# High halves of two weight blocks ahead of their low halves, and a later place for the output function, in the paired products of a streaming-encoder block

## The chip, the cores and the metric

The kernel runs on one core of one Trainium2 chip. The metric is the device time of one execution in microseconds. Three runs of the kernel before took 1686.04, 1686.25 and 1686.39 us; the median is 1686.25. One more execution was recorded by the hardware profiler; all rows below come from it.

The engines are named as in the profile: PE is TensorE's matmul, PEld its weight load, DVE is VectorE, ACT is ScalarE, POOL is GpSimd, SP is SyncE. PEq, SPq, ACTq and POOLq are the sequencers and DMA queues of these engines. L259 is line 259 of the kernel before.

## The reference

One layer of a block on 512 tokens with 2048 channels, all in float32:

```python
h = rmsnorm(x, norm_gain)
proj = h @ w_in
(aq, ak, av, az, iq, ik, iw, rq, rk, rv, rz, ga, gb) = jnp.split(proj, SPLIT_POINTS, axis=-1)
...
a_out = dsa_mixer(aq, ak, av, iq, ik, iw, positions, rel_bias) * jax.nn.silu(az)
...
b_out = retention_mixer(rq, rk, rv, ret_gn_gain) * jax.nn.silu(rz)
merged = jax.nn.sigmoid(ga) * (a_out @ w_a_out) + jax.nn.sigmoid(gb) * (b_out @ w_b_out)
r = x + merged @ w_o
return r + (p_i @ w_ple) * jax.nn.sigmoid(r @ w_ple_gate)
```

`dsa_mixer` is an attention over the top 128 keys of an index score, with a relative bias; `retention_mixer` is a chunkwise retention with rotary queries and keys. A last rmsnorm follows. What matters here is that most of the time goes into plain products of a 2048-wide activation with weight matrices: `w_in` in many column blocks, then `w_a_out`, `w_b_out`, `w_o` and `w_ple_gate`.

## The kernel before, in words

Activations lie with channels on the 128 partitions and the 512 tokens along the free axis. A float32 product is made from rounded parts: a value v is split into a high part (a copy to a rounded type, on ScalarE) and a low part (v minus the high part, on VectorE). `split_to` (L122) does this for weights: ScalarE writes `wh` (L137), and a function `rest` writes `wl` on VectorE (L142). `rest` may also change the raw weights for a later use: it adds another raw block (L144, VectorE) or starts an accumulating load from memory (L105, issued by POOL). `wh` and `wl` have three buffers each, the raw weights seven.

Column blocks are computed two at a time by `gemm_pair` (L214), by a scheme of seven products in place of eight (a Strassen form): the inner dimension has two halves, the two column blocks are the two column halves, and the tokens are the two row halves. The seven weight combinations are units 0 to 6 of the pair, made from four raw blocks in place: `t` is used for units 0, 4 and 5 with sums in between, `w11` for 1 and 6, `w21` for 2, `w22` for 3. The activation side (`X`) has been made before. Each product has eight k steps. A step has one matmul with the high weights over 512 columns (256 of the activation's high part and 256 of its low part) and one with the low weights over 256 columns. Products 0 to 6 accumulate in the banks v, p, q, r, p, v, p of the accumulator memory, where 4, 5 and 6 add to what is there already.

The order of TensorE's work is written out by hand: for each product in turn the eight high matmuls, then the eight low ones; in products 4 and 6 the low ones come first. After a product, its bank is copied by ScalarE (`pv`, `e1`, `e2`, `e3`, L225) or combined with such a copy by VectorE (`out`, L229), and `done` adds the 256-column pieces into the output tiles (L887). There are 40 pairs with `gate_pair` (24 for retention's queries and keys and the merge gates, four for the retention gate, eight for attention's queries and keys, four for its gate) and eight with `w_o`; the first of the eight (`late`) takes the last k step of products 0 and 1 after the others, since its operand is made last.

Every two matmuls `step` (L161) counts a tick. Work that other engines are to do is put into the program at a tick: `later(n, f)` runs `f` n ticks on, `todo` gives one piece a tick, and `bg` one piece every so many ticks (top-k rounds, masks of the bias). A product has eight ticks, a pair 56. Ticks only fix the order in each engine's queue: each engine works through its queue in order and waits where an operand or a buffer is not there yet.

At the start of product n, `split_to` puts the split of the weights two products ahead into the queues, and `load_to` issues raw loads (SyncE, L116) up to seven units ahead. `rest` follows one tick later. When both pieces of an output tile are there, `gate_pair` puts `finish` into the queue one tick later. `finish` is an activation function on ScalarE with a store on ScalarE's own DMA queue (L896, L923), for the retention gate a product and a store on POOL (L910 to L912), and in the pairs of retention's queries and keys a rotation (`rotate`): two copies on ScalarE (L757, L758) and, three, five and seven ticks later, three operations on VectorE (L759 to L761). From the second rotation on retention's own small matmuls are counted (at 24, 39, 51 and 90 ticks after it).

Of the kernel before, what the change touches and what calls it, by code (L numbers as in the profile page):

```python
# [35 lines left out]
def block_kernel(tc, xT, pT, posb, posq, w_in, w_v, w_ik, w_a, w_b, w_o, w_ple, w_gate,  # L36
                 w_gt, w_pt, fgb, tab, gains, cst, dec, out, out_a, out_b):
    nc = tc.nc
    pe, dve, act, pool, sp = nc.tensor, nc.vector, nc.scalar, nc.gpsimd, nc.sync

    with contextlib.ExitStack() as ctx:
# [10 lines left out]
        def U(name, dt=F32):  # L52
            return up.tile([128, L], dt, name=name, tag="u")

        def B(name, dt=F32):
            return bp.tile([128, 1280], dt, name=name, tag="b")

        def P(name):
            return pp.tile([128, L], F32, name=name, tag="p")
# [10 lines left out]
        loaded = {}  # L70
# [29 lines left out]
        def view(t, nk, cols):  # L100
            return t.rearrange("p a c -> p (a c)")[:, 0:nk * cols].rearrange("p (a c) -> p a c", c=cols)

        def add_block(r, b):
            src, k0 = b
            pool.dma_start(out=raw_tiles[r], in_=src[:, k0:k0 + 8, :], accum_op=OP.add)  # L105

        def load_to(n):
            need = max((u[0] for u in units[:n]), default=-1) + 1
            while state["raw"] < need:
                i = state["raw"]  # L110
                src, k0, nk, cols, plus = raws[i]
                if nk * cols <= L and i < 4:
                    t = U("wraw4").rearrange("p (a c) -> p a c", c=128)
                else:
                    t = wp.tile([128, 8, 128], F32, name="wraw", tag="wraw", bufs=RAW_BUFS)
                sp.dma_start(view(t, nk, cols), src[:, k0:k0 + nk, :])  # L116
                raw_tiles[i] = t
                if plus is not None:
                    add_block(i, plus)
                state["raw"] += 1  # L120

        def split_to(n):  # L122
            while state["split"] < min(n, len(units)):
                i = state["split"]
                load_to(i + 1)
                r, plus, nk, cols = units[i]
                if r in unfinished:
                    unfinished[r]()
                raw = view(raw_tiles[r], nk, cols)
                if i in in_raws:  # L130
                    t = wp.tile([128, 2, 512], F32R, name="whl", tag="wraw", bufs=RAW_BUFS)
                    h, l = t[:, 0:1], t[:, 1:2]
                elif nk * cols == L:
                    h, l = (U(n, F32R).rearrange("p (a c) -> p a c", c=cols) for n in ("wh4", "wl4"))
                else:
                    h, l = (view(wp.tile([128, 8, 128], F32R, name=n, tag=n), nk, cols) for n in ("wh", "wl"))
                act.activation(h, raw, AF.Copy)  # L137

                def rest(r=r, plus=plus, l=l, raw=raw, h=h):
                    if unfinished.pop(r, None) is None:  # L140
                        return
                    dve.tensor_sub(l, raw, h.bitcast(F32))  # L142
                    if isinstance(plus, int):
                        dve.tensor_add(raw, raw, view(raw_tiles[plus], nk, cols))  # L144
                    elif plus is not None:
                        add_block(r, plus)

                unfinished[r] = rest
                later(1, rest)
                loaded[i] = (h, l)  # L150
                state["split"] += 1

# [6 lines left out]
        def later(n, f):  # L159
            if n <= 0:  # L160
                return f()  # L161
            tick[1] += 1
            heapq.heappush(soon, (tick[0] + n, tick[1], f))

        def step():
            tick[0] += 1
            while soon and soon[0][0] <= tick[0]:
                heapq.heappop(soon)[2]()
            f = todo.popleft() if todo else None
            if f is not None:  # L170
                f()
            elif bg and tick[0] % state["rate"] == 0:
                bg.popleft()()
# [31 lines left out]
        ALL = slice(0, L)  # L205
# [4 lines left out]

        LO, HI = slice(0, 256), slice(256, 512)
        PRODUCTS = ("s3", "a11", "a12", "s4", "s2", "a22", "s1")

        def gemm_pair(ids, X, done, late=False):  # L214

            p, v, q, r = (P("ps_" + n) for n in ("p", "v", "q", "r"))  # L220
            E = {}

            def copy(n, src):
                E[n] = U(n)
                act.activation(E[n], src, AF.Copy)  # L225

            def out(f, x, y, i, c):
                t = U("e_t")
                f(t, x, y)  # L229
                done(t[:, LO], t[:, HI], i, c)  # L230

            def last():
                copy("e3", p)
                out(dve.tensor_sub, p, E["pv"], 1, HI)
                out(dve.tensor_add, r, E["e3"], 1, LO)

            after = {
                0: lambda: copy("pv", v),
                1: lambda: copy("e1", p),
                2: lambda: out(dve.tensor_sub, q, E["e1"], 0, LO),  # L240
                4: lambda: copy("e2", p),
                5: lambda: out(dve.tensor_sub, v, E["e2"], 0, HI),
                6: last,
            }
            banks = (v, p, q, r, p, v, p)
            runs = [(n, range(8), True) for n in range(7)]
            if late:
                runs[0:2] = [(n, range(7), False) for n in (0, 1)] + [(n, (7,), True) for n in (0, 1)]
            count = 0
            for n, ks, end in runs:  # L250
                i, o = ids[n], banks[n]
                if ks[0] == 0:
                    split_to(i + AHEAD - (late and n == 1))
                    load_to(i + AHEAD + LOADS)
                parts = (1, 0) if n in (4, 6) else (0, 1)
                for part in parts:
                    w, c = loaded[i][part], (ALL, LO)[part]
                    for k in ks:
                        pe.matmul(o[:, c], w[:, k], X[PRODUCTS[n]][k][:, c], start=(n < 4 and part == 0 and k == 0),  # L259
                                  stop=(part == parts[1] and k == 7), skip_group_check=True)  # L260
                        count += 1
                        if count % 2 == 0:
                            step()
                if end and n in after:
                    after[n]()

        def combos(lo, hi, name, keep=None):


            X = {n: [None] * 8 for n in PRODUCTS}  # L270
            T = {}
# [138 lines left out]

        x_split(0)
        split_to(1)
        step()
        x_split(1)
# [254 lines left out]
        hd = dp.tile([56, 128, L], F32, name="hd")  # L669
        x_at = {(n, k): hd[8 * i + k] for i, n in enumerate(PRODUCTS) for k in range(8)}  # L670
        xn = {}
# [10 lines left out]
        _, h_step = combos(lambda k: xn[k], lambda k: xn[k + 8], "h", lambda n, k: x_at[n, k])  # L682
# [168 lines left out]

        Xh = {n: [None] * 8 for n in PRODUCTS}
        x_wanted = collections.deque((n, k) for n in PRODUCTS for k in range(8))

# [25 lines left out]
        def gate_pair(ids, finish):  # L880
            t = B("go")
            outs = [t[:, 0:512], t[:, 512:1024]]
            have = [0, 0]

            def done(c0, c1, i, q):
                o = outs[i]
                dve.tensor_add(o[:, q], c0, c1)  # L887
                have[i] += 1
                if have[i] == 2:
                    later(1, lambda: finish(i, o))  # L890

            gemm_pair(ids, Xh, done)

# [195 lines left out]
        for m in PAIRED:  # L1089
            t = B("sm")  # L1090
            s, o = t[:, 0:512], t[:, 512:1024]
# [17 lines left out]
        for m in range(8):  # L1109
# [9 lines left out]
            def done(c0, c1, i, q, xc=xc):  # L1119
                dve.tensor_add(xc[i][:, q], xc[i][:, q], c0)  # L1120
                dve.tensor_add(xc[i][:, q], xc[i][:, q], c1)
# [14 lines left out]
        for m in range(MF):  # L1136
            i = u_p[m // 4][0]
# [5 lines left out]
            for k in range(2):  # L1143
                a, b = pparts[k]
                w = 2 * (m % 4) + k
# [129 lines left out]
        for i in range(2):  # L1275
            c = (slice(0, 384), slice(384, 512))[i]
# [16 lines left out]
        for q in range(MF // 4):  # L1293
            o = U("yo")
# [6 lines left out]
            o = o.rearrange("p (a c) -> p a c", a=4)  # L1301
# [9 lines left out]
AHEAD = 3  # L1311
LOADS = 5
# [101 lines left out]
```

## Time and profile before

| What | Value |
|---|---|
| median of three runs | 1686.25 us |
| lowest and highest run | 1686.04 and 1686.39 us |
| the profiled execution | 1686.46 us |
| span of the profiled execution, first to last instruction | 1684.7 us |
| mean granted TensorE clock | 0.998 |
| instructions | 24747 |
| stage of the 40 gate pairs | from about 279 us to about 1110 us |
| stage of the eight `w_o` pairs | from about 1318 us to about 1477 us |

How to read the rows. The page gives each engine's busy time with its share of the span, and the chain of work that ended last, followed back from the last instruction, as shares. A row of a group has line, engine, operation, output<-inputs, shapes and count; behind the first bar the busy time in us and the mean of one in ns; behind the second the engine's idle time just before these instructions and what ended it. A row of the timeline has start, length, engine, line, operation, tiles and count of like instructions in a row; a bracket tells of idle time before it and what ended it. Matmuls are pipelined, so the length of a row reaches into the next one, and the pace is read from start to start. A row of the chain has start, length and what, a product's high and low matmuls together (x16); its starts lie a little later than those of the timeline.

### The profile page before, as it was taken

The numbers are of one execution on the slowest core, as the hardware profiler recorded it, in microseconds if no ns is written. First come the engines' busy times: TensorE is split into PE (matmuls) and PEld (weight loads), VectorE is DVE, ScalarE is ACT, GpSimd is POOL, SyncE is SP. The second block draws the span as 40 slices with busy tenths as digits, with TensorE's granted clock in tenths as the row PEclk, the third lists the DMA queues.
The fourth block names the chain that finished last, engine by engine and source line by source line (L and its number), as shares of the span: only waits on it lengthen the run. The fifth ranks groups of instructions, "written<-read, shape, count | busy, mean of one in ns | idle before, by whom it ended". The sixth has DMA issues, their size and how long they took to land.

```text
span 1684.7 us, 24747 instructions
## 1 busy us (share of the span) xinstructions
PE 1672.4 (99%) x9208; PEld 1451.1 (86%) x9208; DVE 1275.3 (76%) x2020; ACT 863.0 (51%) x1278; POOL 214.8 (13%) x216
## 2 busy tenths in 40 slices
PE   9999999999999999999999999999999999999997
PEld 7988888888888888888888888888888888888897
DVE  7797888987878878877876876787768877864453
ACT  7465423555555555555554555566644444463342
POOL 2100000111111111111331111100000111112222
PEclk9999999999999999999999999999999999999999
DMA  7438989788788788788988889898566788733222
GB/s 288 126 107 310 374 298 327 182 229 220 183 219 213 200 215 212 198 213 215 250 237 214 217 206 233 246 368 278 177 200 189 193 229 214 204 116 100 88 63 100
DMA packets 135369, 355.85 MB, mean 211 GB/s; under 512 B 14801, under 2 KB 26961, under 8 KB 135249
## 3 DMA queue, kind: packets, MB, share of 16 engines
q1 hardware_dynamic: 102496, 256.20, 44.3%
q0 software_dynamic: 21376, 77.60, 25.5%
q10 hardware_dynamic: 11376, 20.47, 3.3%
q8 instruction: 72, 1.18, 0.3%
q14 instruction: 49, 0.39, 0.1%
HBM read 301.26 MB, written 52.95 MB: 210 GB/s over the span
## 4 chain that ended last, share of the span: by engine, by line
PE 94%; DVE 2%; ACT 1%; DMA 1%; issue 1%; POOL 0%; SPq 0%; POOLq 0%; ACTq 0%; DVEq 0%
PE ps_p L259 23%; PE ps_v L259 16%; PE ps_r L259 8%; PE ps_q L259 8%; PE ps_vn L726 3%; PE ps_vn L727 3%; PE ps_vn L728 3%; PE ps_w L198 3%; PE ps_w L197 3%; PE ps_w L199 3%; PE ps_pg L199 3%; PE ps_pg L197 3%; PE ps_pg L198 3%; PE ps_iq L197 1%; PE ps_iq L199 1%; PE ps_iq L198 1%
## 5 line engine op out<-in xcount | busy, mean ns | idle before, releaser
L142 DVE TENSOR_TENSOR wl<-wraw,wh 128x1024 fp32r<-128x1024 f32 (+2 forms) x459 | 562.1, 1232 | 201.7 <-ACT wh L137 198.4
L137 ACT ACTIVATE wh<-wraw 128x1024 fp32r<-128x1024 f32 (+2 forms) x459 | 474.1, 1042 | 283.5 <-DVE wraw L144 129.3
L105 POOL DMA_DIRECT2D wraw<-w_in x120 | 106.3, 960 | 837.6 <-DVE wl L142 264.3
L225 ACT ACTIVATE e<-ps_p 128x512 f32<-128x512 f32 x144 | 86.1, 598 | 158.6 <-PE ps_p L259 151.5
L259 PE MATMUL ps_p<-hs,wh 128*128 128x512 f32 x640 | 161.3, 394 | 0.0
L259 PEld LDWEIGHTS ps_p<-hs,wh 128*128 128x128 f32 x640 | 114.9, 189 | 21.2 <-issue 0.7
L726 PE MATMUL ps_vn<-wh,hh 128*128 128x512 f32 x256 | 99.8, 390 | 0.0
L727 PE MATMUL ps_vn<-wl,hh 128*128 128x512 f32 x256 | 99.7, 390 | 0.0
L728 PE MATMUL ps_vn<-wh,hl 128*128 128x512 f32 x256 | 99.7, 389 | 0.0
L259 PE MATMUL ps_p<-hs,wl 128*128 128x256 f32 x640 | 92.0, 284 | 0.7 <-DVE wl L142 0.7
L259 PEld LDWEIGHTS ps_p<-hs,wl 128*128 128x128 f32 x640 | 83.0, 192 | 1.4 <-DVE wl L142 0.9
L259 PE MATMUL ps_r<-hs,wh 128*128 128x512 f32 x320 | 82.2, 395 | 0.0
L259 PE MATMUL ps_v<-ha,wh 128*128 128x512 f32 x320 | 80.6, 393 | 0.0
L259 PE MATMUL ps_p<-ha,wh 128*128 128x512 f32 x320 | 80.4, 393 | 0.0
L259 PE MATMUL ps_q<-ha,wh 128*128 128x512 f32 x320 | 80.1, 392 | 0.0
L259 PE MATMUL ps_v<-hs,wh 128*128 128x512 f32 x320 | 79.6, 390 | 0.1
L199 PE MATMUL ps_pg<-rh,wl 128*128 128x512 f32 x192 | 74.8, 390 | 0.0
L197 PE MATMUL ps_pg<-rh,wh 128*128 128x512 f32 x192 | 74.7, 389 | 0.0
L198 PE MATMUL ps_pg<-rl,wh 128*128 128x512 f32 x192 | 74.7, 389 | 0.0
L887 DVE TENSOR_TENSOR go<-e_t 128x256 f32<-128x256 f32 x160 | 68.1, 425 | 5.6
L259 PEld LDWEIGHTS ps_v<-hs,wh 128*128 128x128 f32 x320 | 59.8, 188 | 13.2 <-ACT wh L137 0.5
L259 PEld LDWEIGHTS ps_v<-ha,wh 128*128 128x128 f32 x320 | 59.3, 188 | 12.5 <-issue 0.5
(361 smaller groups left out, 3499.4 us busy)
## 6 DMA issues: line engine op xcount, KB each, us to landing
wraw<-w_in SPq DMA_DIRECT2D x172, 512.0 KB, 5.5
wraw<-w_in POOLq DMA_DIRECT2D x120, 512.0 KB, 8.4
wraw<-w_v SPq DMA_DIRECT2D x32, 512.0 KB, 5.0
wraw<-w_o SPq DMA_DIRECT2D x32, 512.0 KB, 5.1
wraw<-w_o POOLq DMA_DIRECT2D x24, 512.0 KB, 6.7
wraw<-w_gate SPq DMA_DIRECT2D x24, 512.0 KB, 4.1
hd<-hs SPq DMA_DIRECT2D x32, 256.0 KB, 5.2
hs<-hd SPq DMA_DIRECT2D x32, 256.0 KB, 5.4
```

What stands on the lines that cost most here:

```text
L105: pool.dma_start(out=raw_tiles[r], in_=src[:, k0:k0 + 8, :], accum_op=OP.add)
L137: act.activation(h, raw, AF.Copy)
L142: dve.tensor_sub(l, raw, h.bitcast(F32))
L197: pe.matmul(o, h[:, k, w], a, start=(s == order[0]), stop=False)
L198: pe.matmul(o, h[:, k, w], b, start=False, stop=False)
L199: pe.matmul(o, l[:, k, w], a, start=False, stop=(s == order[-1]))
L225: act.activation(E[n], src, AF.Copy)
L259: pe.matmul(o[:, c], w[:, k], X[PRODUCTS[n]][k][:, c], start=(n < 4 and part == 0 and k == 0), stop=(part == parts[1] and k == 7), skip_gr ...
L726: pe.matmul(pss[t], a[:, tok(t)], h[:, k], start=(s == 0), stop=False)
L727: pe.matmul(pss[t], a[:, tok(t)], l[:, k], start=False, stop=False)
L728: pe.matmul(pss[t], b[:, tok(t)], h[:, k], start=False, stop=(s == KT - 1))
L887: dve.tensor_add(o[:, q], c0, c1)
```

## The change

In `gemm_pair` the high matmuls of products 0 and 1 come first, then their low ones; the same for products 2 and 3. Products 4, 5 and 6 keep their order. The places at which splits are put into the queues are a table (`SPLIT_AT`, by number of the run of eight matmuls), and so are those of the loads. The split for product 3 stands ahead of the low matmuls of product 0, with its low half five ticks behind instead of one. The split for product 5 stands ahead of the low matmuls of product 3, where it stood ahead of the high ones. In the pair marked `late` the last k step of products 0 and 1 follows the same order. In `gate_pair` the function on a finished tile comes five ticks behind the last sum instead of one.

```diff
-        def split_to(n):
+        def split_to(n, lag=1):
...
-                later(1, rest)
+                later(lag, rest)
...
+        RUNS = [(n, part) for part, ns in enumerate(((0, 1), (0, 1), (2, 3), (2, 3, 4), (4, 5), (5, 6), (6,)))
+                for n in ns]
+        RUNS = [(n, part % 2) for n, part in RUNS]
+
+        SPLIT_AT = {0: 3, 2: 4, 3: 4, 4: 5, 7: 6, 8: 7, 10: 8, 12: 9}
+        LOAD_AT = (0, 2, 4, 6, 8, 10, 12)
...
-            runs = [(n, range(8), True) for n in range(7)]
+            runs = [(n, part, range(8)) for n, part in RUNS]
             if late:
-                runs[0:2] = [(n, range(7), False) for n in (0, 1)] + [(n, (7,), True) for n in (0, 1)]
+                runs[0:4] = [(n, part, ks) for ks in (range(7), (7,)) for n, part, _ in runs[0:4]]
+            ended = [0] * 7
             count = 0
-            for n, ks, end in runs:
+            for at, (n, part, ks) in enumerate(runs):
+                at = max(at - 4, 0) if late else at
                 i, o = ids[n], banks[n]
-                if ks[0] == 0:
-                    split_to(i + AHEAD - (late and n == 1))
-                    load_to(i + AHEAD + LOADS)
-                parts = (1, 0) if n in (4, 6) else (0, 1)
-                for part in parts:
-                    w, c = loaded[i][part], (ALL, LO)[part]
-                    for k in ks:
-                        pe.matmul(o[:, c], w[:, k], X[PRODUCTS[n]][k][:, c], start=(n < 4 and part == 0 and k == 0),
-                                  stop=(part == parts[1] and k == 7), skip_group_check=True)
-                        count += 1
-                        if count % 2 == 0:
-                            step()
-                if end and n in after:
+                if at in SPLIT_AT and not (late and at == 2):
+                    split_to(ids[0] + SPLIT_AT[at], 5 if at == 2 else 1)
+                if at in LOAD_AT:
+                    load_to(ids[LOAD_AT.index(at)] + AHEAD + LOADS)
+                w, c = loaded[i][part], (ALL, LO)[part]
+                first = ended[n] == 0
+                for k in ks:
+                    ended[n] += 1
+                    pe.matmul(o[:, c], w[:, k], X[PRODUCTS[n]][k][:, c], start=(n < 4 and first and k == 0),
+                              stop=(ended[n] == 16), skip_group_check=True)
+                    count += 1
+                    if count % 2 == 0:
+                        step()
+                if ended[n] == 16 and n in after:
                     after[n]()
...
                 if have[i] == 2:
-                    later(1, lambda: finish(i, o))
+                    later(5, lambda: finish(i, o))
```

## The prediction

> **What bounds the kernel now.** I read the busy shares on the page first, then the chain of work that ended last, then the groups of instructions.
>
> ```profile
> PE 1672.4 (99%) x9208; PEld 1451.1 (86%) x9208; DVE 1275.3 (76%) x2020; ACT 863.0 (51%) x1278; POOL 214.8 (13%) x216
> ...
> PE 94%; DVE 2%; ACT 1%; DMA 1%; issue 1%; POOL 0%; SPq 0%; POOLq 0%; ACTq 0%; DVEq 0%
> ...
> L142 DVE TENSOR_TENSOR wl<-wraw,wh 128x1024 fp32r<-128x1024 f32 (+2 forms) x459 | 562.1, 1232 | 201.7 <-ACT wh L137 198.4
> ```
>
> TensorE is busy 99% of the span and carries 94% of the chain. VectorE comes next, at 76%, and its largest work is the low halves of weights (L142). The reader is to see that only two things can move the time: TensorE's own pace, and a new wait of TensorE for a weight half. The view of line 259, the products of a pair, tells how much waiting there is to remove:
>
> ```profile
>   issue: 3.0, 9
>   DVE wl L142: 1.9, 3
>   ACT wh L137: 0.5, 1
>   DVE e_t L229: 0.4, 1
> ```
>
> That is under 6 us over 48 pairs, weight loads counted beside the matmuls. So the first part of the change has to be judged by the pace of matmuls that never wait. The timeline of TensorE over one pair with no other matmuls in it:
>
> ```profile
> 868.17 1.98 PE L259 MATMUL ps_v<-hs,wh 128*128 128x512 f32 x8
> 869.98 1.11 PE L259 MATMUL ps_v<-hs,wl 128*128 128x256 f32 x8
> 870.93 2.00 PE L259 MATMUL ps_p<-ha,wh 128*128 128x512 f32 x8
> 872.78 1.11 PE L259 MATMUL ps_p<-ha,wl 128*128 128x256 f32 x8
> 873.73 2.00 PE L259 MATMUL ps_q<-ha,wh 128*128 128x512 f32 x8
> ...
> 879.32 1.12 PE L259 MATMUL ps_p<-hs,wl 128*128 128x256 f32 x8
> 880.27 2.00 PE L259 MATMUL ps_p<-hs,wh 128*128 128x512 f32 x8
> 882.12 1.98 PE L259 MATMUL ps_v<-ha,wh 128*128 128x512 f32 x8
> 883.93 1.12 PE L259 MATMUL ps_v<-ha,wl 128*128 128x256 f32 x8
> ```
>
> Matmuls overlap, so a run of eight is measured from its start to the start of the next. A high run behind a high run (868.17, and 882.12) takes 1.81 us. A high run behind a low run (870.93) takes 1.85 and (880.27) 1.85. Low runs take 0.95 us behind a high run (869.98, 872.78) and as much behind a low one (879.32). So what a run costs depends a little on its neighbour. These differences are near the last digit of the view; the chain over the same pair adds a high and a low run in each row and serves as a second reading:
>
> ```profile
> 865.53 2.80 PE ps_p L259 x16
> 868.33 2.77 PE ps_v L259 x16
> 871.10 2.79 PE ps_p L259 x16
> 873.89 2.79 PE ps_q L259 x16
> 876.68 2.79 PE ps_r L259 x16
> 879.48 2.80 PE ps_p L259 x16
> 882.28 2.77 PE ps_v L259 x16
> 885.04 2.80 PE ps_p L259 x16
> ```
>
> From 871.10 to 879.48 three products, each a high run behind a low one and a low run behind a high one, take 8.38 us, 2.793 each. The products at 868.33 and 882.28 (high behind high, low behind high) take 2.77 and 2.76, mean 2.765. Those at 865.53 and 879.48 (low behind low, then high behind low) take 2.80 each.
>
> **The order of the runs.** Name a run by product and half: 0h is the high run of product 0. Before: 0h 0l 1h 1l 2h 2l 3h 3l 4l 4h 5h 5l 6l 6h. After: 0h 1h 0l 1l 2h 3h 2l 3l and then the same six. No matmul is added or taken away. Runs 1h and 3h come to stand behind a high run instead of a low one: by the chain each gains 2.793 - 2.765 = 0.028 us. Runs 1l and 3l come to stand behind a low run instead of a high one: each loses 2.80 - 2.793 = 0.007. Net 0.02 us for each of two places in 48 pairs: 2 x 48 x 0.02 = **1.9 us** off the path. The bounds are those of the readings: by single chain rows, 0.02 - 0.01 gives 0.01 a place and 1.0 us in all; by the timeline, 0.03 to 0.04 less nothing gives up to 3.8 us. I take 0.02, from the longest stretch.
>
> The Trainium skill, "TensorE: Matmul & The Clock Gate", Part 2, Step-by-step (① LDWEIGHTS), speaks against this part: the next weights load while this matmul runs, over a read port of their own, so a matmul's neighbours would not matter and the order would be worth nothing. The 1.81 beside 1.85 us above speaks against the rule at this fine a scale.
>
> **The splits that move.** With the 1.81, 1.85 and 0.95 us above, 3h starts 7.4 us after its pair's start instead of 8.4 and 1h 1.8 instead of 2.8: their high halves must be there 1 us earlier. Low run 2l starts 9.2 us in instead of 7.4, so that low half has more time, and 4l to 6h keep theirs. What the halves have to spare, from ScalarE's timeline of the same pair and VectorE's:
>
> ```profile
> 868.86 1.05 ACT L137 ACTIVATE wh<-wraw 128x1024 fp32r<-128x1024 f32 x1
> 871.25 0.63 ACT L910 ACTIVATE go<-go 128x512 f32<-128x512 f32 x1 [1.33 <-DVE go L887]
> 871.78 0.58 ACT L225 ACTIVATE pv<-ps_v 128x512 f32<-128x512 f32 x1
> 872.26 1.05 ACT L137 ACTIVATE wh<-wraw 128x1024 fp32r<-128x1024 f32 x1
> ...
> 884.13 1.06 ACT L137 ACTIVATE wh<-wraw 128x1024 fp32r<-128x1024 f32 x1 [0.27 <-PE ps_v L259]
> ```
>
> ```profile
> 873.58 1.21 DVE L142 TENSOR_TENSOR wl<-wraw,wh 128x1024 fp32r<-128x1024 f32 x1
> ```
>
> The high half for 3h (872.26) is done at 873.31, 5.1 us into the pair. After the change it even stands ahead of the copy `pv` (0.58 us) in ScalarE's queue. Spare: at least 7.4 - 5.1 = 2.3 us. That for the next pair's 1h (884.13) is done at 885.19 and wanted at 868.17 + 19.5 (the seven rows of the chain from 868.33 on) + 1.81 = 889.5, 4.3 us later. The low half for 3l is moved five steps back. In its buffer lies the low half of product 0, which TensorE now reads until about 4.6 us into the pair (1.81 + 1.81 + 0.95) instead of 2.8. VectorE gets to it at 873.58, 5.4 us in, so that the new wait has passed; behind it stand the low half for 4l and the sum `t += w21`, for which the split for 5h waits. Cost in such pairs: nothing; were VectorE to come 1 us earlier it would wait a little, and start the work at the same time as today. SyncE's and POOL's queues keep their order: raw loads go out at seven places as before (two of them 0.9 us later in program order, several us ahead of use), and the accumulating loads on POOL hang on the low halves for products 0 and 1, whose places stay.
>
> **The function, five steps back.** On ScalarE it stands behind the same split as before and ahead of the same next one (steps 1 to 5 hold no other work of that engine in a plain pair), so it waits the same 1.33 us for VectorE. Its store on ScalarE's queue moves along. Worth: nothing, hidden by TensorE. Only the eight pairs behind the rotary ones differ, where it is a rotation with three multiplications on VectorE. Timelines of VectorE, ScalarE and TensorE in one of these (the pair that starts at 681.56):
>
> ```profile
> 681.72 0.69 DVE L759 TENSOR_TENSOR go<-go,ct 128x512 f32<-128x512 f32 x1 [0.21 <-ACT rb L758]
> ...
> 683.66 0.68 DVE L229 TENSOR_TENSOR e_t<-ps_p,pv 128x512 f32<-128x512 f32 x1
> ...
> 691.12 1.22 DVE L142 TENSOR_TENSOR wl<-wraw,wh 128x1024 fp32r<-128x1024 f32 x1
> ```
>
> ```profile
> 687.74 1.05 ACT L137 ACTIVATE wh<-wraw 128x1024 fp32r<-128x1024 f32 x1
> ```
>
> ```profile
> 689.91 0.63 PE L259 MATMUL ps_r<-hs,wh 128*128 128x512 f32 x2
> ...
> 693.93 0.28 PE L259 MATMUL ps_p<-hs,wl 128*128 128x256 f32 x1
> ```
>
> Here 4l has 693.93 - 692.34 = 1.6 us to spare and 3h 689.91 - 688.79 = 1.1. With the lag, two of the first tile's multiplications (683.66 less the end of the first, 682.41, is 1.25 us) fall behind the pair's six closing sums; the sums start 1.25 us earlier, and the two multiplications fill the time in which VectorE would wait for the second tile's copies. The backlog is the same at the low half for 4l. For 3h the rotation's copies come 1.2 us earlier too, so the split does. Cost: nothing, with 1.6 us as cover.
>
> In the first pair of the `w_o` stage, which keeps the last k of products 0 and 1 for later, the last of 1h comes one low matmul earlier (0.95 / 8 = 0.12 us); its operand is then done 0.08 us ahead instead of 1323.81 - 1323.61 = 0.20, so this costs nothing:
>
> ```profile
> 1323.19 0.42 DVE L279 SCALAR_TENSOR_TENSOR ma<-sm,ma 128x256 fp32r<-128x256 f32 x1
> ...
> 1323.81 0.40 PE L259 MATMUL ps_p<-ma,wh 128*128 128x512 f32 x1
> ```
>
> Retention's own matmuls move four steps with the rotation. Its last eight now stand at the joint of two pairs, which takes 0.03 us of high behind high from eight pairs; the ones ahead of 5h go behind it and give as much back: 0.
>
> **Stalls that are there.** The second pair waits for the low half of 4l:
>
> ```profile
> 310.95 1.22 DVE L142 TENSOR_TENSOR wl<-wraw,wh 128x1024 fp32r<-128x1024 f32 x1
> ```
>
> ```profile
> 312.23 1.21 PE L259 MATMUL ps_p<-hs,wl 128*128 128x256 f32 x8 [0.72 <-DVE wl L142]
> ```
>
> VectorE has this pair's top-k work in front of it. The stall stays; I estimate 0.2 us more, since two pieces of VectorE's work no longer pack without a gap. A gain of the whole 0.7 and a loss of 1 us are the bounds.
>
> **The sum.** -1.9 + 0.2 = -1.7 us. The profiled execution took 1686.46 us (span 1684.7, 1.8 us around it) and stands 0.2 above the median 1686.25; taken from the median: **1684.5 us**, 0.10% less. Two medians of this kernel less than 0.2% (3.4 us) apart I call the same.
>
> **The rivals.** (1) *The order is worth nothing*, as the skill's rule has it: 1686.2 us. Chance 0.15; against it stand both readings of eight rows. (2) *Slower: backlog of VectorE in the eight rotary pairs.* If the displaced multiplications do not fill VectorE's wait but come after it, VectorE stands still for 1.25 us ahead of the sums and for another 1.3 us (two copies of about 0.6) ahead of the second tile's. That is 2.55 us late at the low half for 4l, against a cover of 1.6; from 1.6 us on it decides, and each further tenth costs 0.8 us over eight pairs. Price 8 x 0.95 = 7.6, time 1684.5 + 7.6 = 1692.1. Chance 0.13, and 0.02 for more of it. For it speaks that the cover is the least of all; against it, that 1.4 us of work with no wait stands between. (3) *Faster: the pace at its upper bound and the waits gone too:* 3.8 + 0.7 = 4.5 off, 1681.7. Chance 0.08. My forecast has 0.62.
>
> Range 1682.8 to 1688.0: the pace's bounds without (3), rival (1), and a part of (2) up to 3.5 us, which leaves out about 0.2. Faster by over 0.2%: 0.08; within: 0.77; slower: 0.15.
>
> **What would show it.** Right: a pair without other matmuls takes 0.04 us less; runs 1h and 3h take 1.81; L259 idles no more than 6 us; waits of ScalarE for VectorE's sums stay. Wrong: rows of 3h or 4l with an idle time before them, released by L137 or L142; a 1h run of 1.85 us in spite of its neighbour; low runs that grow longer once sixteen stand in a row.

## The result and the profile after

The kernel after takes 1688.17 us (median of 21 runs, 1686.97 to 1689.85), the kernel before 1686.04 beside it (median of 21 runs). The ratio is 1.0012, 95% interval 1.0007 to 1.0018: slower by 2.1 us, where 1.7 us less was forecast, and 0.2 us above the upper end of the range. By the prediction's bound of 0.2% it is "the same", but the interval leaves out both no change and the forecast (0.9990). The profiled execution took 1689.85 us, span 1688.1, 3.4 us more than the span before. It is the longest of the 21 runs, so it is likely to hold more waiting than the median run.

The page after: busy time by engine, the chain, and the group of the low halves.

```profile
PE 1671.8 (99%) x9208; PEld 1451.4 (86%) x9208; DVE 1275.9 (76%) x2020; ACT 864.5 (51%) x1278; POOL 214.5 (13%) x216
...
PE 48%; issue 2%; DVE 2%; DMA 2%; ACT 1%; POOL 0%; POOLq 0%; SPq 0%; ACTq 0%; DVEq 0%
...
L142 DVE TENSOR_TENSOR wl<-wraw,wh 128x1024 fp32r<-128x1024 f32 (+2 forms) x459 | 561.0, 1231 | 211.5 <-ACT wh L137 201.5
```

The same instructions take the same time on every engine: PE 0.6 us less, VectorE 0.6 more. The chain is no help here; its shares add up to 55%, so it cannot be set beside the 94% of before. What did change is waiting. The view of the products of a pair (now line 267), time in which TensorE sat idle before them, in us and times, by what ended it:

```profile
  DVE wl L142: 8.5, 10
  issue: 3.0, 9
  ACT wh L137: 1.2, 3
  DVE ma L287: 0.2, 1
```

Waits for a low half went from 1.9 us to 8.5. The view counts weight loads beside the matmuls, so the same wait can stand in it twice. Counted once, as the time from one matmul's start to the next beyond the usual pace, between the matmuls of the pairs, TensorE's gaps went from 1.7 us to 6.0. By place, those 6.0 us are 1.46 in the second pair; 1.09, 0.38, 0.66, 1.42, 0.18 and 0.30 ahead of 4l in six pairs, one in every three (the gaps begin at 354.8, 419.4, 483.4, 547.6, 612.6 and 676.1 us), 4.0 together; 0.46 at 3h of a pair of the retention gate; 0.10 in the first `w_o` pair.

From its first to its last product of a pair the kernel took 1195.3 us before and 1197.9 after: 2.7 more, which is some 4.4 of new gaps less some 1.7 by which the products themselves became faster. The other 0.7 of the span lie ahead of the first pair. In the twelve traces kept, that first pair starts anywhere from 278.4 to 279.9 us, so these 0.7 are not put down to the change.

The order did what was forecast. The chain over a pair with no other matmuls in it, start, length and runs of eight:

```profile
872.89 1.81 PE ps_v L267 x8
874.70 1.81 PE ps_p L267 x8
876.52 0.95 PE ps_v L267 x8
877.47 0.96 PE ps_p L267 x8
878.43 1.84 PE ps_q L267 x8
880.27 1.81 PE ps_r L267 x8
882.08 0.95 PE ps_q L267 x8
883.04 0.96 PE ps_r L267 x8
884.00 2.80 PE ps_p L267 x16
886.80 2.77 PE ps_v L267 x16
889.56 2.80 PE ps_p L267 x16
```

Runs 1h (874.70) and 3h (880.27), now behind a high run, take 1.81; 2h, behind a low one, takes 1.84. Runs 1l and 3l take 0.96 behind a low run where 0l and 2l take 0.95 behind a high one. The pair takes 889.56 + 2.80 - 872.89 = 19.47 us; before, it was 19.52 from 868.33 to the next `ps_v` row at 887.85. So 0.05 us less by these rounded rows. By the starts of the matmuls, the median of the 21 pairs with no other matmuls in them went from 19.513 to 19.474 us: 0.04 less, as forecast.

So something else gave the gain back, at 4l, in one pair of three. The pairs with a gap are pairs of retention's queries and keys, and each comes right behind the pair in which the step `back` ends the head before. `back` turns that head's result round (`yT`, ScalarE, L843 before and L851 after) and stores it (`yd`, L844 and L852) through SyncE's queue. ScalarE's rows around one such joint of two pairs, before, with `yT` and with the split for unit 4 of the next pair:

```profile
526.71 0.67 ACT L843 ACTIVATE yT<-ps_t,g_sb 128x512 f32<-128x512 f32 x1
...
540.23 1.06 ACT L137 ACTIVATE wh<-wraw 128x1024 fp32r<-128x1024 f32 x1
```

SyncE's queue there, before:

```profile
527.41 0.33 SPq L844 DMA_DIRECT2D yd<-yT  x1
527.78 1.41 SPq L116 DMA_DIRECT2D wraw<-w_in  x3
```

POOL's queue, before; its DMA is the accumulating load that turns `t` into the weights of that unit 4:

```profile
531.83 0.95 POOL L105 DMA_DIRECT2D wraw<-w_in  x1 [11.03 <-DVE mk L640]
```

The same two queues after, and the time to landing of that one load, before and then after:

```profile
533.38 0.33 SPq L852 DMA_DIRECT2D yd<-yT  x1
533.76 1.39 SPq L116 DMA_DIRECT2D wraw<-w_in  x3
```

```profile
534.45 0.95 POOL L105 DMA_DIRECT2D wraw<-w_in  x1 [12.65 <-DVE mk L648]
```

```profile
DMA to landing us min/median/max: 7.4/7.4/7.4
```

```profile
DMA to landing us min/median/max: 12.2/12.2/12.2
```

Three raw loads stand behind the store, which waits for `yT`. Before, they left 531.83 - 527.78 = 4.1 us ahead of the accumulating load; after, 0.7 us ahead. Beside them that load needs 12.2 us instead of 7.4. The other five joints whose next pair shows a gap are alike: 11.0 to 11.9 us after, 7.0 to 8.4 before. Before, it landed at 531.83 + 7.4 = 539.2, 1.0 us ahead of its split (540.23, with no wait). What waits now, one engine after the other, ScalarE, VectorE and TensorE after:

```profile
531.24 0.60 ACT L230 ACTIVATE e<-ps_p 128x512 f32<-128x512 f32 x1 [2.65 <-PE ps_p L267]
531.73 1.05 ACT L137 ACTIVATE wh<-wraw 128x1024 fp32r<-128x1024 f32 x1
532.68 0.68 ACT L851 ACTIVATE yT<-ps_t,g_sb 128x512 f32<-128x512 f32 x1
...
546.69 1.06 ACT L137 ACTIVATE wh<-wraw 128x1024 fp32r<-128x1024 f32 x1 [3.71 <-DMA wraw<-w_in]
```

```profile
547.78 1.23 DVE L142 TENSOR_TENSOR wl<-wraw,wh 128x1024 fp32r<-128x1024 f32 x1 [4.66 <-ACT wh L137]
```

```profile
549.06 0.50 PE L267 MATMUL ps_p<-hs,wl 128*128 128x256 f32 x2 [1.16 <-DVE wl L142]
```

Read it from the end: 4l waits for its low half, that for the high half, that for the load (534.45 + 12.2 = 546.7). The page's view names only VectorE as the releaser; the cause lies four steps further back. The first three rows tell why `yT` is late: it starts 1.8 us ahead of the accumulating load instead of 5.1. Four ticks on, it stands in ScalarE's queue behind the copy `e` of product 4, which waits 2.65 us for TensorE, and behind one more split.

The Trainium skill, "DMA: Bandwidth & Descriptors", "Issuing engines are not separate DMA queues", says that transfers begun by ScalarE, SyncE and GpSimd end up on the same 16 DMA engines and interleave. The 7.4 and 12.2 us agree with it.

### The profile page after: what moved, and what is told of

It is laid out like the page before. It is cut to its first block, busy times and chain, and to the rows that moved or that the text cites. A ratio compares the mean times of both kernels' runs of the same rounds, so it can differ in the third digit from the quotient of the medians.

```text
span 1688.1 us, 24748 instructions
## 1 busy us (share of the span) xinstructions
PE 1671.8 (99%) x9208; PEld 1451.4 (86%) x9208; DVE 1275.9 (76%) x2020; ACT 864.5 (51%) x1278; POOL 214.5 (13%) x216
## 4 chain that ended last, share of the span: by engine, by line
PE 48%; issue 2%; DVE 2%; DMA 2%; ACT 1%; POOL 0%; POOLq 0%; SPq 0%; ACTq 0%; DVEq 0%
PE ps_p L267 11%; PE ps_v L267 7%; PE ps_r L267 4%; PE ps_q L267 4%; PE ps_w L198 3%; PE ps_w L197 3%; PE ps_w L199 3%; PE ps_pg L199 3%; PE ps_pg L197 3%; PE ps_pg L198 3%; DMA wraw<-w_in 1%; PE ps_pg L1233 1%; PE ps_pg L1235 1%; PE ps_pg L1234 1%; ACT bm L984 1%
## 5 line engine op out<-in xcount | busy, mean ns | idle before, releaser
L142 DVE TENSOR_TENSOR wl<-wraw,wh 128x1024 fp32r<-128x1024 f32 (+2 forms) x459 | 561.0, 1231 | 211.5 <-ACT wh L137 201.5
L137 ACT ACTIVATE wh<-wraw 128x1024 fp32r<-128x1024 f32 (+2 forms) x459 | 473.0, 1043 | 329.3 <-DVE wraw L144 115.1
L267 PEld LDWEIGHTS ps_p<-ha,wh 128*128 128x128 f32 x320 | 60.0, 188 | 13.1 <-ACT wh L137 0.4
```

## The experiments

Each time is the median of 5 to 11 runs, beside 20 to 30 runs of the kernel before that were taken with them. Theory A in the expectations is the one above: the four ticks that the rotation is moved delay `yT` and its store, the store holds back the raw loads, and these collide with the accumulating load. The rivals are a VectorE backlog in the rotary pairs (the prediction's second rival) and a loss from the order itself.

**The two parts apart.** First the kernel after with the old place of the function:

```diff
-                    later(5, lambda: finish(i, o))
+                    later(1, lambda: finish(i, o))
```

> The change with its function lag back at one tick (order and split places stay). Theory A (the lag makes retention's store of yT late; it stands ahead of three raw loads in SyncE's queue, these land beside POOL's accumulating load, and 4l of the pairs behind waits for it: 4.0 us of stalls in the profile of the changed kernel; the order itself gives 1.9 us): no idle time before 4l but in the second pair, 1.9 us faster than before, ratio 0.9989. Rival B (the new order or split places make the stalls): stalls at 4l of pairs 4, 7, 10, 13 stay, ratio 1.001.

1684.20 us beside 1685.93, ratio 0.9987 (0.9978 to 0.9996). Then the kernel before with the new place alone:

```diff
-                    later(1, lambda: finish(i, o))
+                    later(5, lambda: finish(i, o))
```

> The kernel before with the function five ticks behind, order and splits as before. Theory A: the stalls of 4l come without the order's gain, about 4.0 us slower than before, ratio 1.0024. Rival B: no new stall, ratio 1.000.

1689.85 us, ratio 1.0021 (1.0012 to 1.0030). The order gives 1.7 us, the lag costs 3.9, together 2.2 slower, and both parts in one kernel measured 2.1. In the order's kernel TensorE's gaps are 1.4 us, all but 0.1 of them in the second pair. With the lag alone the gaps are 3.4 us: 2.1 ahead of 4l in the same pairs as after (417.0, 481.4, 545.6 us and smaller ones) and 1.2 at 2l of a pair of the retention gate, which comes back below. So the order is not what loses. That execution shows 1.7 us of gaps more than before. This count leaves out a wait in the second pair, ahead of retention's own matmuls, which before did not wait there:

```profile
309.54 1.13 PE L775 MATMUL ps_rs<-go 128*128 128x128 f32 x8 [1.02 <-DVE go L761]
```

Here the matmuls that read the rotated tile wait for VectorE's rotation (L761), and the pair's own products no longer do. From the first to the last product this execution takes 3.0 us more than before; its span is only 2.1 longer, because it reached the first pair 0.8 us sooner. It is one of the faster runs of that kernel (1688.56 us), and what the rest of the median's 3.9 us is, about 0.9, was not seen.

**The store alone.** The kernel after, everything in it, with the store of `yT` on ScalarE's DMA queue, where no raw load stands behind it:

```diff
-                    later(2, lambda: sp.dma_start(yd[h], E["yT"]))
+                    later(2, lambda: act.dma_start(yd[h], E["yT"]))
```

> The changed kernel with the store of yT issued on ScalarE's DMA queue instead of SyncE's, so that no raw load stands behind it. Theory A: raw loads go out about 3 us earlier in these pairs, 4l waits no more, 1.9 us faster than before, ratio 0.9989. Rival C (something else of the lag makes the accumulating load late, such as POOL's own queue): stalls stay, ratio 1.001.

1684.33 us beside 1685.93, ratio 0.9990 (0.9981 to 0.9998). The whole loss is gone, with the function still five ticks late and the copy `yT` as late as after, 1.8 us ahead of the accumulating load. The timeline of this kernel at the joint shown above:

```profile
524.08 5.33 SPq L116 DMA_DIRECT2D wraw<-w_in  x3
...
530.96 0.33 ACTq L852 DMA_DIRECT2D yd<-yT  x1
...
532.03 0.95 POOL L105 DMA_DIRECT2D wraw<-w_in  x1 [12.64 <-DVE mk L648]
...
540.52 1.06 ACT L137 ACTIVATE wh<-wraw 128x1024 fp32r<-128x1024 f32 x1
```

The issue of the raw loads begins 8 us ahead of the accumulating load and ends 2.6 us ahead of it; that load lands after 8.5 us, and the split for unit 4 (540.52) no longer waits. The VectorE backlog falls here: the rotation's operations stand in the same places of the program as in the kernel after, and none of the six 4l waits any more.

The control is the kernel before with the same edit, line 844.

> The kernel before with the store of yT on ScalarE's queue and nothing else: a control. Theory A: before, the raw loads leave some 4 us ahead of the accumulating load, so the store is harmless and its queue is worth nothing: ratio 1.000, and the 1.9 us of the runs with the new order are the order's. Rival G (the store's queue alone is worth something): ratio 0.999.

1686.35 us beside 1685.75, ratio 1.0002 (0.9993 to 1.0011). The store's queue is worth nothing by itself where `yT` is early; it only takes the lag's harm away.

**`back` alone.** The kernel before with `back` four ticks later and nothing else:

```diff
-            steps += [(57, norm), (70, scale), (90, lambda: back(0)), (94, lambda: back(1))]
+            steps += [(57, norm), (70, scale), (94, lambda: back(0)), (98, lambda: back(1))]
```

> The kernel before with only the transposition of yn and the copy yT four ticks later (94 and 98 instead of 90 and 94), everything else as before. Theory A: this alone makes the store late behind the copy e2 and the next split, and brings stalls at 4l in about five pairs, 3 to 4 us slower than before, ratio 1.002. Rival C (other parts of the lag do it): ratio 1.000.

1690.31 us beside 1685.93, ratio 1.0024 (1.0014 to 1.0034): as much as the whole lag costs, from one step moved. SyncE's queue and POOL's in this kernel:

```profile
532.41 0.33 SPq L844 DMA_DIRECT2D yd<-yT  x1
532.79 1.40 SPq L116 DMA_DIRECT2D wraw<-w_in  x3
```

```profile
533.48 0.95 POOL L105 DMA_DIRECT2D wraw<-w_in  x1 [11.06 <-DVE mk L640]
```

The same 0.7 us between them, a landing after 11.4 us, and gaps ahead of 4l at the same joints (1.17 us at 481.8, 0.60 at 546.7, 0.48 at 611.0).

**`back` much later.** The kernel before with 110 and 114 in the same line. If a later store only makes it worse (rival E), this is the slowest; if it is the meeting of the loads that costs, it need not be.

> The kernel before with the transposition of yn and the copy yT 20 ticks later (110 and 114) instead of 4 (the run before: 4.4 us slower). Theory A with contention (the three raw loads harm because they start beside the accumulating load): they now start some 5 us behind it, so the stalls at 4l shrink to under half, 0 to 2 us slower than before; raw loads that come too late may wait at 0h of the pair behind. Rival E (the later the store, the later all that stands behind it, and the larger the stall): more than 4.4 us slower, ratio over 1.003.

1685.98 us beside 1685.85, ratio 1.0001 (0.9992 to 1.0009). ScalarE's, SyncE's and POOL's rows in order of time:

```profile
531.50 0.95 POOL L105 DMA_DIRECT2D wraw<-w_in  x1 [10.61 <-DVE mk L640]
...
538.93 0.33 SPq L844 DMA_DIRECT2D yd<-yT  x1
...
539.35 1.95 SPq L116 DMA_DIRECT2D wraw<-w_in  x2
...
540.70 1.07 ACT L137 ACTIVATE wh<-wraw 128x1024 fp32r<-128x1024 f32 x1
```

The store is now 20 ticks late and the two raw loads behind it start 7.9 us after the accumulating load, which lands after 6.4 us. Nothing waits. So it is not lateness that costs but the meeting of the transfers; E falls.

**The rotation alone put back.** The kernel after, where only the pairs of retention's queries and keys keep the old lag:

```diff
-        def gate_pair(ids, finish):
+        def gate_pair(ids, finish, lag=5):
...
-                    later(5, lambda: finish(i, o))
+                    later(lag, lambda: finish(i, o))
...
-            gate_pair(u_r[h], retention(h))
+            gate_pair(u_r[h], retention(h), 1)
```

> The changed kernel with five ticks of lag for all functions but the rotation, which is back at one tick. Theory A (only the rotation's lag harms, by the late store of yT): as the order alone, 1.7 to 1.9 us faster than before, ratio 0.999. Rival D (the lag of the plain functions costs something too): above 1.000.

1684.13 us beside 1685.85, ratio 0.9989 (0.9980 to 0.9998). In the other pairs the lag of five costs nothing, as forecast. It gains nothing either: the order with a lag of one took 1684.20.

**The order with the store on ScalarE's queue**, lag one.

> The order alone (lag of one tick) with the store of yT on ScalarE's queue: a candidate for the fastest. Theory A: the store no longer matters once yT is early; the same as the order alone, 1.7 to 2.2 us faster than before, ratio 0.999. Rival: the raw loads leave earlier still and free other waits, 3 us or more faster, ratio 0.998.

1683.97 us beside 1685.85, ratio 0.9988 (0.9979 to 0.9997), the lowest of all and below both kernels, though not to be told from the order alone (0.9987). The rival's 3 us did not come. The same kernel with the low half for 3l one tick behind its high half, as before, instead of five:

```diff
-                    split_to(ids[0] + SPLIT_AT[at], 5 if at == 2 else 1)
+                    split_to(ids[0] + SPLIT_AT[at])
```

> The order with the function lag back at one tick and the store on ScalarE's queue (as in the run that was the fastest so far, ratio 0.9988), and the low half for product 3 one tick behind its split instead of five. Theory: VectorE gets to it 5.4 us into a pair, after its buffer is free at 4.6, so the place is worth nothing: ratio 0.999, and only the second pair, where top-k work stands near it, may differ by some tenths of a us. Rival F (VectorE then waits for the buffer with other work behind it): 1 us or more slower than that run, ratio 0.9995 or above.

1684.58 us beside 1685.75, ratio 0.9991 (0.9982 to 1.0000). The five ticks for that low half are worth nothing that can be measured. The interval reaches rival F's 0.9995 too; against F stand the traces, in which TensorE's waits in the second pair add up to the same 1.3 us in both kernels.

**The price of a neighbour.** The kernel before with high and low matmuls alternating by k step, the same matmuls in another order:

```diff
-                for part in parts:
-                    w, c = loaded[i][part], (ALL, LO)[part]
-                    for k in ks:
+                for k in ks:
+                    for part in parts:
+                        w, c = loaded[i][part], (ALL, LO)[part]
```

> The kernel before with high and low matmuls alternating at each k step in place of runs of eight: 56 changes from high to low in a pair instead of 5. Reading P1 (each change from low to high costs about 0.02 us): 51 more changes in 48 pairs, about 50 us slower, ratio 1.03. Reading P2 (in the trace of before the first low matmul behind a high one starts its successor after 113 ns instead of 120, the first high one behind a low one after 233 instead of 227: a strict alternation costs 346 ns a pair of matmuls against 347): no dearer than runs of eight, 0 to 6 us faster if no low half comes late, ratio 0.997 to 1.000. Reading P3 (neighbours do not matter): 1.000.

1692.82 us beside 1685.85, ratio 1.0038 (1.0024 to 1.0052): 7.0 us slower, which is none of the three readings. Its chain, whole products:

```profile
886.20 2.78 PE ps_v L259 x16
...
897.40 2.83 PE ps_q L259 x16
900.24 2.82 PE ps_r L259 x16
```

With 16 alternating neighbours, products 1 to 4 of a pair take 2.82 to 2.83 us where two runs of eight took 2.79 to 2.80; product 5 (the first row) takes 2.78 where it took 2.77, and product 6 takes 2.78 where it took 2.80. If each change of neighbour cost the 0.02 us that it costs between runs, all would be 0.3 more. So the effect between runs is real, but it is not a fixed price for each change; what it hangs on inside TensorE these rows do not tell. This kernel's gaps are 2.2 us more than before as well, so not all of its loss is pace.

## Why the prediction was wrong, point by point

- *What bounds the kernel*: right in the main. TensorE's pace and its new waits for a weight half moved the time of the kernel after. Not every wait was for a weight half: with the lag alone, 1.0 us was a wait of retention's own matmuls for the rotation, and about 0.9 us of that kernel's median stay open. What the prediction named as signs of being wrong came: rows of 4l, and one of 3h, with an idle time before them that L142 or L137 ended.
- *The order of the runs, -1.9 us*: right. The order alone measured 1.7 (ratio 0.9987), the pair 0.04 us less. Rival 1 falls with it. The prediction drew from the Trainium skill ("TensorE: Matmul & The Clock Gate", Part 2, Step-by-step) that with the next weights loading while a matmul runs, neighbours would not matter. The 1.81 and 1.84 us do not bear that conclusion out; whether the weight loads make the difference, no run here shows.
- *The splits that move, nothing*: right in sum, with less spare than said. In the pair of the chain above the high half for 3h is done 1.9 us ahead of its use, not 2.3, because the function ahead of it waits longer for VectorE (2.12 us). ScalarE's rows and TensorE's after:

```profile
876.60 0.63 ACT L918 ACTIVATE go<-go 128x512 f32<-128x512 f32 x1 [2.12 <-DVE go L895]
877.13 1.05 ACT L137 ACTIVATE wh<-wraw 128x1024 fp32r<-128x1024 f32 x1
```

```profile
880.11 1.98 PE L267 MATMUL ps_r<-hs,wh 128*128 128x512 f32 x8
```

- *"SyncE's and POOL's queues keep their order"*: true, and the wrong question. The order of the entries did stay, but an entry in the middle, the store of `yT`, became ready later relative to what POOL does, and SyncE's queue stood still for it. What leaves when is set by the entry that waits.
- *"Retention's own matmuls move four steps with the rotation ... 0"*: **this is the step that failed.** I counted TensorE's instructions of the moved step and not the rest of it: the copy `yT` on ScalarE, which falls behind a copy that waits for product 4, and its store. The accumulating load's landing 1.0 us ahead of its split was in the trace of before and would have told how little room there was. In place of 0 stand 4.0 us of gaps in the profiled execution, the longest of its 21 runs (before: none), and 3.9 us between the medians of the lag alone; the store's queue alone took the ratio from 1.0012 to 0.9990.
- *The function five steps back, nothing, "only the eight pairs behind the rotary ones differ"*: right for the plain pairs, wrong on "only". The pairs behind the rotary ones, which it named, show no gap but the second pair's, which was there before, so the VectorE backlog (rival 2, 7.6 us) did not come; a wait for the rotation itself stands in the second pair with the lag alone (1.0 us). The new gaps lie in the rotary pairs after them, where the head's last step ends.
- *The second pair, +0.2 us*: the size about right, 1.17 us before and 1.46 after, but not the place: the wait stands at 3l now, behind its pieces of the top-k work, and not at 4l. So the size is in part luck. TensorE's row after:

```profile
310.92 0.51 PE L267 MATMUL ps_r<-hs,wl 128*128 128x256 f32 x2 [1.19 <-DVE wl L142]
```

- *The first `w_o` pair, nothing*: a miss of 0.1 us. The 0.08 us of spare did not hold (0.2 for `DVE ma L287` in the view above, matmul and weight load together).
- *The rival on the slower side* was looked for on the engine with the least cover, and not in the queue of an idle one. The mechanism that decided stood in none of the three.
- *The function in the pairs of the retention gate, nothing*: a second, smaller miss, 0.46 us at 820 us. The lag moves POOL's product of the function beside an addition on VectorE, and the addition takes 1.5 us longer (last section). All four kernels with a lag of five in these pairs show such an addition (after, the lag alone, the store moved, the rotation put back); of the eight with a lag of one, none does. TensorE waits for it in two of the four, 0.46 us after and 1.2 us with the lag alone; in these two the addition took 1.99 us, in the other two 1.23. The function on ScalarE hangs on VectorE's additions, and the split for 3h stands behind it. ScalarE after:

```profile
818.70 0.63 ACT L918 ACTIVATE go<-go 128x512 f32<-128x512 f32 x1 [3.02 <-DVE go L895]
```

## What to carry to other kernels

When a step is moved, follow everything that hangs on it to its last DMA, and for each queue it enters ask what stands behind it and when that would then leave; a store that waits for a late operand turns into a late load. A store whose operand comes from a long chain belongs in a queue with no prefetch behind it, which here turned a loss of 2.1 us into a gain of 1.6. And where a few tenths of a per cent are at stake, put the two halves of a change on the chip apart: here -1.7 and +3.9 hid behind +2.1.

## What the runs showed of the hardware

An accumulating load of 512 KB, with three raw loads of 512 KB begun within a microsecond of it, took 11.3 to 12.2 us to land in three kernels at the joint shown (after, the lag alone, `back` four ticks later). Where their issue had ended at least 2.6 us ahead of it, or two of them began 7.9 behind, it took 6.4 to 8.5 in four (before, the order alone, the store moved, `back` twenty later). Over the six joints named above and all twelve traces it took 10.8 to 12.2 us in those three kernels and 5.4 to 8.5 in the nine others. What in the transfers stretches it, these runs do not tell.

One addition of 128x256 on VectorE, which takes 0.425 us in the median of 160, took 1.99 while POOL multiplied two tiles. The view of its line: operation, count, and least, median and longest in ns, after, then in the order's kernel with a lag of one; and the two rows of VectorE and POOL after:

```profile
L895 DVE TENSOR_TENSOR go<-e_t x160: 424/425/1991, 291.0 to 1113.1; 128x256 f32<-128x256 f32 x160
```

```profile
L895 DVE TENSOR_TENSOR go<-e_t x160: 424/425/428, 289.8 to 1106.9; 128x256 f32<-128x256 f32 x160
```

```profile
815.61 1.99 DVE L895 TENSOR_TENSOR go<-e_t 128x256 f32<-128x256 f32 x1
815.69 1.62 POOL L919 TENSOR_TENSOR go<-go,y 128x512 f32<-128x512 f32 x1
```

The addition ends 0.29 us behind the product. The four kernels with a lag of five hold twelve such additions, of 1.22 to 1.99 us, and each ends 0.29 us behind the product that it overlaps. The Trainium skill, "SBUF — State Buffer", "SBUF: two separate sides", says that VectorE and GpSimd share a pair of ports to this memory that one of them holds for a whole instruction while the other stands. The ends of the twelve agree with it. In the rows shown the addition starts 0.08 us ahead of the product and is yet the one that stands, so what settles which of the two holds the ports is not shown here; no run took POOL's product away.
